# Moving the split operands of every projection to multiples of 128 bytes, and joining the two halves of a row

## The chip, the cores and the metric

The program runs on one core of a Trainium2 chip. That core has five engines that run side by side and meet at semaphores: TensorE (PE, matrix products; its loading of the stationary operand is listed apart as PEld), VectorE (DVE), ScalarE (ACT), GpSimd (POOL) and SyncE (SP), which here only issues DMAs. The metric is the device time of one execution in microseconds; less is better. The kernel before takes 2662.29 us, the median of three runs (2661.83 to 2664.8).

## What is computed

The reference is a two-layer streaming encoder on 256 tokens of width 2048, all in float32. Layer 0 is an RWKV-7 time mixing, layer 1 a chunked band attention on one shared K/V; each is followed by a squared-ReLU MLP, and each sub-layer sits between an RMS norm with a shift and scale made from `c`, and a gate made from `c`.

```
mod = c @ w_ada[layer] + b_ada[layer];  sh1, sc1, gt1, sh2, sc2, gt2 = split(mod, 6)
h = rms_norm(x, g_mix[layer]) * (1 + sc1) + sh1
y = rwkv7_time_mix(h, ...)  if layer == 0  else  chunk_band_attention(h, kp, vp, w_q, w_o, rel_bias)
x = x + gt1 * y
h = rms_norm(x, g_mlp[layer]) * (1 + sc2) + sh2
x = x + gt2 * (square(relu(h @ w_up[layer])) @ w_down[layer])      # 2048 -> 8192 -> 2048
...
return rms_norm(x, g_final)
```

The weights read are 657 MB, and nearly all work is dense products with a 2048-row weight: the time mixing has four (r, k, v, o), the attention four (shared K, shared V, q, o), and each MLP eight times as much as one of these.

## The kernel before

**How a product is made.** Activations lie with the 128 channels of a block on the partitions and the 256 tokens along the row. TensorE reads an operand of the type float32r, which holds a rounded float32; to keep the precision each operand is split into the rounded part H and the rest L, and a product is made as H·aH + H·aL + L·aH. A weight block of 128 by 1024 floats comes by DMA into a tile `raw` (line 372), ScalarE rounds it into `wH` (line 382), and VectorE writes `raw − wH` into `wL` (line 385). The three tiles have 4096 bytes in each partition.

**The split activations** are kept in two kinds of tile. `aHL` (line 421, from `new_hl`) holds all 16 channel blocks (kt = 0 to 15) of one 2048-wide input; the hidden layer of the MLP has one tile `hHL` for each of its blocks (2 by 256 floats, so 2048 bytes). A row of `aHL` is 258 floats (TE = T + 2), because one of its uses, `new_scaled`, puts the shift as two further columns behind the 256 tokens. So in block kt the rounded half begins 2064·kt bytes into the tile, and the low half another 1032 bytes on, 8 bytes behind the end of the rounded half's 256 tokens. `hHL` has no such gap: its low half lies directly behind the rounded one.

**Two ways to multiply.** `proj2` (lines 416 and 417) sends both halves of an activation as one operand of 512 columns past `wH`, and the rounded half again, 256 columns, past `wL`: two multiplications for each kt, called a *pair* here. `proj` (lines 405 to 407) makes three of 256 columns, a *trio*; it is used where one accumulator of 256 columns must do (the time mixing's r and k and the begun part of its output product), and with 258 columns where the shift's column is wanted (the first eight blocks of each MLP and of the shared K). Lines 773 to 775 and 811 to 813 make the same trios for v. Pairs read `aHL` in the MLP's up products, the attention's four products and most of the time mixing's output product, 2816 in all; they read `hHL` in the MLP's down products, 2048 in all. Trios of 256 columns read `aHL` 896 times, those of 258 columns 384 times.

**What sets the order.** Each engine runs its instructions in the order in which the program lists them. The weight DMAs are issued on SP's queue ahead of use into six `raw` buffers; the split weights have three buffers each; the products of a stage follow each other block by block. Between the products VectorE adds up the shift, scale and gate vectors from the tiles `rada` and `raw` (line 458, one 128 by 1024 piece at a time), so in the first MLP and the attention TensorE also does small sums of these (line 480).

**Where tiles lie.** Tiles are placed one behind the other in each partition, in the order in which the pools and tiles are opened, each start rounded up to 32 bytes. The small tile `ct` (the 16 columns of `c`, 64 bytes) is opened near the front, ahead of all large ones except the constants. As the program is placed, the starts are these (bytes, modulo 128):

| tiles | before | after |
|---|---|---|
| `raw`, `wH`, `wL`, `acc`, `rada` (4096 bytes) | 96 | 0 |
| `hHL` (2048 bytes) | 96 | 0 |
| `aHL` (33024 bytes), block kt | 96 + 16·kt, low half 8 more | 0 for both halves; with width 258: 16·kt, low half 8 more |
| tiles of the time mixing's inner work | 32 | 64 |
| `x` and the tiles of the norms outside the time mixing | 96 | 96 |

The stationary operand of kt is 512·(kt mod 8) bytes into its `wH` or `wL` tile, so it has the tile's start modulo 128 too.

Of the kernel before, what the change touches and what calls it, by code (L numbers as in the profile page):

```python
# [12 lines left out]
F32 = mybir.dt.float32  # L13
F32R = mybir.dt.float32r
# [4 lines left out]
P = 128  # L19
D = 2048  # L20
T = 256
KT = D // P
# [7 lines left out]
TE = T + 2  # L30
# [303 lines left out]
class Body:  # L334
# [82 lines left out]
            ins = nc.tensor.matmul(ps[:, 0, :], L[:, i, :], a(kt)[:, 0, :], start=False, stop=(kt == KT - 1))  # L417
        return ins.ins

    def new_hl(self):  # L420
        return self.hp.tile([P, KT, 2, TE], F32R, tag="aHL", bufs=2, name="aHL")


    def ada_src(self, layer, part):
# [131 lines left out]

    def new_scaled(self, sh):
        nc = self.nc
        hl = self.new_hl()
        H, L = hl[:, :, 0, T:TE], hl[:, :, 1, T:TE]  # L560
        s = sh.unsqueeze(2).to_broadcast([P, KT, TE - T])
        nc.scalar.copy(H, s)
        nc.vector.tensor_tensor(out=L, in0=s, in1=H, op=ALU.subtract)
        return hl
# [13 lines left out]
    def run(self):  # L578
        nc, tc, d = self.nc, self.tc, self.d
        ctx = self.ctx  # L580
        gp = self.gp = ctx.enter_context(tc.tile_pool(name="gp", bufs=1))
        self.wp = ctx.enter_context(tc.tile_pool(name="wp", bufs=2))
        nc.scalar.preload_act_table_set("natural_log_exp_and_others")
        self.hp = ctx.enter_context(tc.tile_pool(name="hp", bufs=2))
        self.csts = gp.tile([P, CST.shape[1]], F32, name="csts")
        self.vecs = gp.tile([P, len(VECS), KT], F32, name="vecs")
        self.bada = gp.tile([P, 2 * 96 + 32], F32, name="bada")
        self.ct = gp.tile([P, KT], F32, name="ct")
        nc.scalar.dma_start(out=self.ct, in_=d["c"])
        self.mods = {}  # L590
        for layer in (0, 1, "kv"):
            for part in range(2 if layer == 0 else 0, 2 if layer == "kv" else 6):
                self.mods[(layer, part)] = gp.tile([P, KT], F32, name=f"mod_{layer}_{part}")
        self.mods01 = gp.tile([P, 2, KT], F32, name="mods01")
        for part in range(2):
            self.mods[(0, part)] = self.mods01[:, part, :]
        self.nhalf, self.pool_every = 0, 0
        self.lazy, self.fins, self.ada_pool = False, iter(()), None
        self.ada_done = set()
        self.adas, self.ada_q = self.ada_tiles(), deque()  # L600

        sv, sp = ExitStack(), ExitStack()
        v = self.layer_a(sv, sp)
        with ExitStack() as st:
            self.np = st.enter_context(tc.tile_pool(name="npl", bufs=1, side="right", reuse_waits="tile"))
            xp = st.enter_context(tc.tile_pool(name="xp", bufs=1, side="right", reuse_waits="tile"))
            self.x = xp.tile([P, KT, T], F32, name="x")
            for j in range(KT - 2, KT):
                self.split(self.y_hl, j, v[:, j, :])
            sv.close()  # L610
            self.ada_need((0, 2), (0, 4), (0, 3))
            nxt = self.out_proj(self.pp, "w_o", self.y_hl, (0, 2), "g_mlp0", (0, 4), (0, 3), self.o_ps)
            sp.close()
            with ExitStack() as s2:
                pp = s2.enter_context(tc.tile_pool(name="ps_m0", bufs=2, space=bass.MemoryType.PSUM, reuse_waits="tile"))
                self.psm = lambda: pp.tile([P, 512], F32, tag="m", bufs=2, name="m")
                s2.enter_context(self.ada_room(5))
                nxt = self.mlp(s2, pp, 0, *nxt, "g_kv", ("kv", 1), ("kv", 0))
            with ExitStack() as s2:
                pp = s2.enter_context(tc.tile_pool(name="ps_at", bufs=2, space=bass.MemoryType.PSUM, reuse_waits="tile"))  # L620
                self.psm = lambda: pp.tile([P, 512], F32, tag="m", bufs=1, name="m")
                s2.enter_context(self.ada_room(3))
                o_hl = self.attention(s2, pp, *nxt)
                self.ada_need((1, 2), (1, 4), (1, 3))
                nxt = self.out_proj(pp, "attn_w_o", o_hl, (1, 2), "g_mlp1", (1, 4), (1, 3))
            with ExitStack() as s2:
                pp = s2.enter_context(tc.tile_pool(name="ps_m1", bufs=2, space=bass.MemoryType.PSUM, reuse_waits="tile"))
                self.psm = lambda: pp.tile([P, 512], F32, tag="m", bufs=2, name="m")
                s2.enter_context(self.ada_room(5))
                self.mlp(s2, pp, 1, *nxt)  # L630
                r = self.rstd()
                for lo, hi, eng in ((0, 4, nc.vector), (11, 14, nc.gpsimd), (4, 8, nc.vector), (8, 11, nc.vector),
                                    (14, KT, nc.gpsimd)):
                    x = self.x[:, lo:hi, :]
                    eng.tensor_tensor(out=x, in0=x, in1=r.unsqueeze(1).to_broadcast([P, hi - lo, T]), op=ALU.mult)
                    (nc.sync if eng is nc.vector else nc.scalar).dma_start(out=d["out"][:, lo:hi, :], in_=x)
# [603 lines left out]
```

## Time and profile before

| what | value |
|---|---|
| median of three runs | 2662.29 us (2661.83 to 2664.8) |
| the profiled execution's own time | 2658.25 us |
| its span, first to last instruction | 2656.5 us |
| mean granted TensorE clock | 0.991 |
| TensorE busy | 2577.0 us, 97% |
| VectorE busy | 2094.6 us, 79% |
| ScalarE busy | 1367.6 us, 51% |
| DMA | 663.20 MB, mean 250 GB/s |

The profile comes from one execution, 4 us below the median of the runs. A line of its groups gives the source line, the engine, the operation, the tile written and those read, partitions by elements, the count, the busy time, the mean length of one and the idle time ahead of it with what ended that. Multiplications overlap in the array and their ends are modelled, so the mean lengths of a group (397 ns and 281 ns for the two of a pair) add up to more than the time between one pair and the next; that time is read from the starts in the timeline, or from how many pairs fall into a stretch.

### The profile page before, as it was taken

The numbers are of one execution on the slowest core, as the hardware profiler recorded it, in microseconds if no ns is written. First come the engines' busy times: TensorE is split into PE (matmuls) and PEld (weight loads), VectorE is DVE, ScalarE is ACT, GpSimd is POOL, SyncE is SP. The second block draws the span as 40 slices with busy tenths as digits, with TensorE's granted clock in tenths as the row PEclk, the third lists the DMA queues.
The fourth block names the chain that finished last, engine by engine and source line by source line (L and its number), as shares of the span: only waits on it lengthen the run. The fifth ranks groups of instructions, "written<-read, shape, count | busy, mean of one in ns | idle before, by whom it ended". The sixth has DMA issues, their size and how long they took to land.

```text
span 2656.5 us, 59241 instructions
## 1 busy us (share of the span) xinstructions
PE 2577.0 (97%) x24108; PEld 2253.7 (85%) x24108; DVE 2094.6 (79%) x3054; ACT 1367.6 (51%) x2484; POOL 212.1 (8%) x338
## 2 busy tenths in 40 slices
PE   7999999999999999999999999999999999999997
PEld 4788888888899888888888998877898888888886
DVE  6789878878789888888888898899887556556555
ACT  3346555555456445355365554565564464453554
POOL 1002223223110000000001100000100000000002
PEclk9999999999999999999999999999999999999998
DMA  9876656565768888889998779887766555555553
GB/s 352 311 246 226 203 181 194 184 201 190 248 238 304 328 313 321 328 324 336 325 328 294 238 246 328 316 277 261 264 215 240 188 187 190 190 190 190 185 189 119
DMA packets 207665, 663.20 MB, mean 250 GB/s; under 512 B 21408, under 2 KB 55072, under 8 KB 207392
## 3 DMA queue, kind: packets, MB, share of 16 engines
q1 hardware_dynamic: 205328, 656.89, 71.6%
q8 instruction: 189, 3.10, 0.5%
q10 hardware_dynamic: 2064, 2.53, 0.3%
q14 instruction: 84, 0.69, 0.1%
HBM read 657.23 MB, written 2.10 MB: 248 GB/s over the span
## 4 chain that ended last, share of the span: by engine, by line
PE 81%; DVE 7%; DMA 4%; issue 4%; ACT 2%; POOL 1%; SPq 0%; DVEq 0%; ACTq 0%; POOLq 0%
PE pj L416 42%; PE pj L417 21%; PE pj L405 3%; PE pj L406 3%; PE pj L407 3%; DMA raw<-w_ada 2%; DVE wL L385 2%; DVE acc L458 2%; PE iv L111 1%; PE ms L328 1%; ACT wH L382 1%; DMA raw<-w_o 1%; PE pT L1128 0%; PE o L405 0%; PE m L480 0%
## 5 line engine op out<-in xcount | busy, mean ns | idle before, releaser
L385 DVE TENSOR_TENSOR wL<-raw,wH 128x1024 fp32r<-128x1024 f32 x772 | 942.2, 1222 | 347.0 <-ACT wH L382 340.1
L382 ACT CAST wH<-raw 128x1024 fp32r<-128x1024 f32 x772 | 805.6, 1045 | 761.9 <-PE pj L416 588.9
L416 PE MATMUL pj<-aHL,wH 128*128 128x512 f32 x2816 | 998.1, 397 | 1.4 <-DVE x L953 1.4
L417 PE MATMUL pj<-aHL,wL 128*128 128x256 f32 x2816 | 791.7, 281 | 0.2 <-DVE wL L385 0.2
L416 PE MATMUL pj<-hHL,wH 128*128 128x512 f32 x2048 | 713.8, 395 | 0.0
L416 PEld LDWEIGHTS pj<-aHL,wH 128*128 128x128 f32 x2816 | 532.0, 189 | 129.1 <-issue 8.6
L417 PE MATMUL pj<-hHL,wL 128*128 128x256 f32 x2048 | 568.7, 278 | 0.0
L417 PEld LDWEIGHTS pj<-aHL,wL 128*128 128x128 f32 x2816 | 531.5, 189 | 1.6 <-issue 0.8
L416 PEld LDWEIGHTS pj<-hHL,wH 128*128 128x128 f32 x2048 | 384.1, 188 | 90.1
L417 PEld LDWEIGHTS pj<-hHL,wL 128*128 128x128 f32 x2048 | 384.9, 188 | 0.6 <-DVE wL L385 0.5
L458 DVE SCALAR_TENSOR_TENSOR acc<-rada,ct,acc 128x1024 f32<-128x1024 f32 x256 | 327.9, 1281 | 8.2 <-DMA rada<-w_ada 7.7
L405 PE MATMUL pj<-aHL,wH 128*128 128x256 f32 (+1 forms) x896 | 263.3, 294 | 0.1
L406 PE MATMUL pj<-aHL,wH 128*128 128x256 f32 (+1 forms) x896 | 254.9, 285 | 0.0
L407 PE MATMUL pj<-aHL,wL 128*128 128x256 f32 (+1 forms) x896 | 253.7, 283 | 0.0
L522 POOL TENSOR_TENSOR ss<-ss,sq 128x256 f32<-128x256 f32 x56 | 54.6, 974 | 1579.6 <-ACT sq L521 1579.3
L405 PEld LDWEIGHTS pj<-aHL,wH 128*128 128x128 f32 x896 | 170.7, 190 | 5.0 <-issue 0.5
L407 PEld LDWEIGHTS pj<-aHL,wL 128*128 128x128 f32 x896 | 171.2, 191 | 0.2
L406 PEld LDWEIGHTS pj<-aHL,wH 128*128 128x128 f32 x896 | 170.7, 191 | 0.5
L1024 DVE SCALAR_TENSOR_TENSOR x<-pj,mod,x 128x256 f32<-128x256 f32 x256 | 123.4, 482 | 55.0 <-PE pj L417 51.9
L458 DVE SCALAR_TENSOR_TENSOR acc<-raw,ct,acc 128x1024 f32<-128x1024 f32 x104 | 138.5, 1331 | 19.4 <-DMA raw<-w_ada 19.2
L996 ACT ACTIVATE t<-t 128x256 f32<-128x256 f32 x112 | 46.8, 418 | 124.2 <-DVE t L968 124.2
L998 ACT ACTIVATE t<-t 128x256 f32<-128x256 f32 x128 | 53.4, 417 | 3.4
(252 smaller groups left out, 2818.0 us busy)
## 6 DMA issues: line engine op xcount, KB each, us to landing
raw<-w_up SPq DMA_DIRECT2D x256, 512.0 KB, 4.3
raw<-w_down SPq DMA_DIRECT2D x256, 512.0 KB, 4.3
rada<-w_ada SPq DMA_DIRECT2D x209, 512.0 KB, 5.7
raw<-w_ada SPq DMA_DIRECT2D x111, 512.0 KB, 4.4
rada<-w_ada_kv SPq DMA_DIRECT2D x64, 512.0 KB, 6.6
rawa<-w_ada SPq DMA_DIRECT2D x32, 512.0 KB, 6.8
rawa<-w_ada_t SPq DMA_DIRECT2D x32, 512.0 KB, 7.5
raw<-w_k SPq DMA_DIRECT2D x32, 512.0 KB, 3.8
```

Source lines behind the costliest of these rows:

```text
L382: nc.scalar.copy(Hf, raw)
L385: eng.tensor_tensor(out=Lf, in0=raw, in1=Hf, op=ALU.subtract)
L405: nc.tensor.matmul(ps, H[:, i, :], a(kt)[:, 0, :], start=(first and kt == 0), stop=False)
L406: nc.tensor.matmul(ps, H[:, i, :], a(kt)[:, 1, :], start=False, stop=False)
L407: ins = nc.tensor.matmul(ps, L[:, i, :], a(kt)[:, 0, :], start=False, stop=(last and kt == KT - 1))
L416: nc.tensor.matmul(ps, H[:, i, :], a(kt), start=(kt == 0), stop=False)
L417: ins = nc.tensor.matmul(ps[:, 0, :], L[:, i, :], a(kt)[:, 0, :], start=False, stop=(kt == KT - 1))
L458: nc.vector.scalar_tensor_tensor(out=self.acc, in0=raw, scalar=ck, in1=self.acc, op0=ALU.mult, op1=ALU.add)
L522: (eng or nc.gpsimd).tensor_tensor(out=self.ss, in0=self.ss, in1=sq, op=ALU.add)
L996: nc.scalar.activation(t, t, AF.Relu)
L998: nc.scalar.activation(t, t, AF.Square)
L1024: nc.vector.scalar_tensor_tensor(out=x, in0=ps[:, i, :], scalar=self.mods[(layer, 5)][:, n:n + 1], in1=x, op0=ALU.mult, op1=ALU.add)
```

## The change

`new_hl` takes the width of a row. It is 256 floats unless `new_scaled` asks for 258; the tile has the same size as before (33024 bytes), with the rows of 256 packed into its front. So the low half lies directly behind the rounded half, and the two halves of a block are one run of 2048 bytes. `ct` becomes 24 floats wide (96 bytes), of which the first 16 are used, so every tile that is opened after it moves up by 32 bytes, and the large ones start at the multiples of 128 that the table shows. Nothing else changes: on each engine the same instructions stand in the same order with the same waits, and every operand has the same number of elements; what differs is where the operands lie.

```diff
-    def new_hl(self):
-        return self.hp.tile([P, KT, 2, TE], F32R, tag="aHL", bufs=2, name="aHL")
+    def new_hl(self, width=T):
+        t = self.hp.tile([P, KT * 2 * TE], F32R, tag="aHL", bufs=2, name="aHL")
+        return t[:, :KT * 2 * width].rearrange("p (k i t) -> p k i t", i=2, t=width)
...
     def new_scaled(self, sh):
         nc = self.nc
-        hl = self.new_hl()
+        hl = self.new_hl(TE)
...
-        self.ct = gp.tile([P, KT], F32, name="ct")
+        self.ct = gp.tile([P, KT + 8], F32, name="ct")[:, :KT]
```

## The prediction

> **What bounds the kernel now.** I read the page first: the busy times, the slices and the costliest groups, then the stretches of single stages, then the timeline of TensorE inside one of them.
>
> ```profile
> span 2656.5 us, 59241 instructions
> PE 2577.0 (97%) x24108; PEld 2253.7 (85%) x24108; DVE 2094.6 (79%) x3054; ACT 1367.6 (51%) x2484; POOL 212.1 (8%) x338
> PE   7999999999999999999999999999999999999997
> PEclk9999999999999999999999999999999999999998
> ```
>
> TensorE is busy in nine tenths or more of every slice but the first and the last, at nearly its full clock. What stands in front of a multiplication is in the groups:
>
> ```profile
> L416 PE MATMUL pj<-aHL,wH 128*128 128x512 f32 x2816 | 998.1, 397 | 1.4 <-DVE x L953 1.4
> L417 PE MATMUL pj<-aHL,wL 128*128 128x256 f32 x2816 | 791.7, 281 | 0.2 <-DVE wL L385 0.2
> L416 PE MATMUL pj<-hHL,wH 128*128 128x512 f32 x2048 | 713.8, 395 | 0.0
> L417 PE MATMUL pj<-hHL,wL 128*128 128x256 f32 x2048 | 568.7, 278 | 0.0
> ```
>
> These are the 4864 pairs, and in total 1.6 us of waiting stands ahead of them. So for most of the span only one thing counts: how far apart the multiplications start. No instruction is added, removed or moved by this change; if the time moves, it is because an operand at another address is read or written at another speed. The trace of before holds two natural experiments on that, since the rows of `aHL` start at sixteen different places and those of `hHL` at one.
>
> The first is the second MLP, whose stages do nothing but pairs. The rows give the stretch, its length and the busy time and count of each engine. Up, down, up and down follow each other:
>
> ```profile
> core 0: us, PE busy (x) PEld busy (x) DVE busy (x) ACT busy (x) POOL busy (x), PEclk, DMA share, GB/s
> 2103.50:2193.20 89.70, 89.70 (x514) 78.38 (x513) 50.07 (x64) 53.27 (x92) 0.00 (x0) 1.00 0.56 188
> 2193.20:2282.05 88.85, 88.85 (x514) 77.62 (x513) 53.99 (x65) 34.88 (x36) 0.00 (x0) 1.00 0.57 190
> 2282.05:2371.78 89.73, 89.73 (x514) 78.43 (x513) 50.08 (x64) 53.28 (x92) 0.00 (x0) 1.00 0.56 188
> 2371.78:2460.63 88.85, 88.85 (x514) 77.63 (x513) 53.98 (x65) 34.87 (x36) 0.00 (x0) 1.00 0.56 190
> ```
>
> Each stage is 256 pairs (512 multiplications and one or two at the cut) with TensorE busy throughout. An up stage, which reads `aHL`, takes 89.73 us, or 350.5 ns a pair; a down stage, which reads `hHL`, takes 88.85 us, or 347.1 ns. Same weights' tiles, same number of columns, 3.4 ns apart.
>
> The second is inside an up stage. This is the timeline of TensorE over one weight block of 16 kt; the first row is kt 0, and the others shown are, in order, kt 2, 3, 4 (both of its multiplications), 5, 6, 7, 10, 11, 14, 15 (both), and kt 0 of the next block:
>
> ```profile
> 2304.51 0.39 PE L416 MATMUL pj<-aHL,wH 128*128 128x512 f32 x1
> ...
> 2305.20 0.39 PE L416 MATMUL pj<-aHL,wH 128*128 128x512 f32 x1
> ...
> 2305.55 0.39 PE L416 MATMUL pj<-aHL,wH 128*128 128x512 f32 x1
> ...
> 2305.90 0.39 PE L416 MATMUL pj<-aHL,wH 128*128 128x512 f32 x1
> 2306.12 0.28 PE L417 MATMUL pj<-aHL,wL 128*128 128x256 f32 x1
> 2306.24 0.40 PE L416 MATMUL pj<-aHL,wH 128*128 128x512 f32 x1
> ...
> 2306.60 0.40 PE L416 MATMUL pj<-aHL,wH 128*128 128x512 f32 x1
> ...
> 2306.95 0.40 PE L416 MATMUL pj<-aHL,wH 128*128 128x512 f32 x1
> ...
> 2308.01 0.40 PE L416 MATMUL pj<-aHL,wH 128*128 128x512 f32 x1
> ...
> 2308.37 0.40 PE L416 MATMUL pj<-aHL,wH 128*128 128x512 f32 x1
> ...
> 2309.42 0.40 PE L416 MATMUL pj<-aHL,wH 128*128 128x512 f32 x1
> ...
> 2309.78 0.39 PE L416 MATMUL pj<-aHL,wH 128*128 128x512 f32 x1
> 2310.01 0.28 PE L417 MATMUL pj<-aHL,wL 128*128 128x256 f32 x1
> 2310.12 0.39 PE L416 MATMUL pj<-aHL,wH 128*128 128x512 f32 x1
> ```
>
> The block takes 5.61 us, 350.6 ns a pair, but not evenly: kt 0 to 4 take 2306.24 − 2304.51 = 1.73 us, 346 ns each; kt 5 to 10 take 2308.37 − 2306.24 = 2.13 us, 355 ns each; kt 11 to 15 take 1.75 us, 350 ns each. The engines beside TensorE do not know of kt, so where a row starts matters by some ten nanoseconds a pair, in no order that I can read off as a plain rule of multiples.
>
> **The change, part by part.**
>
> *Rows of `aHL` become runs of 2048 bytes at one alignment.* This is what `hHL` is already: both halves joined, every row at the same place against the stationary operand of its kt. Before, an `aHL` row starts 16 bytes further along against its weights with each kt; after, the distance is the same for all, and it is the one that `hHL` has before and after. So I take the down stage's 347.1 ns for the pairs that read `aHL`: 2816 × 3.44 ns = 9.7 us. It lies on the path in full, since TensorE has no cover there: it is the bound, and nothing else waits to take its place (VectorE is busy 50 of 90 us in these stages; where it is busiest its row is below).
>
> *Trios of 256 columns*, 896 of them, get the same joined rows. The timeline has three such starts in a quiet moment of the time mixing:
>
> ```profile
> 515.57 0.28 PE L405 MATMUL pj<-aHL,wH 128*128 128x256 f32 x1
> 515.69 0.28 PE L406 MATMUL pj<-aHL,wH 128*128 128x256 f32 x1
> 515.81 0.28 PE L407 MATMUL pj<-aHL,wL 128*128 128x256 f32 x1
> 515.93 0.28 PE L405 MATMUL pj<-aHL,wH 128*128 128x256 f32 x1
> ```
>
> That is 360 ns a trio. The trace has no trio on joined rows. The nearest row is the pair's, 1% (3.44 of 350.5); so 3.5 ns × 896 = 3.1 us, with ends of 3.1 us worse (the low half's own multiplication may as well lose) and 6.2 us better (it may gain twice, being the one whose start moves most).
>
> *The 384 trios of 258 columns* keep rows of 258, which move against their weights as before: nothing, ± 1% of 384 × 0.36 us, so ± 1.4 us.
>
> *All large tiles move by 32 bytes.* This shifts moving and stationary operands together. No pair in the trace has weights at another start, so the price is unknown, and bounded from both sides by the slow and fast places of the `aHL` rows (rivals, below). I take nothing: kt 2 and 10 have the rounded half of `aHL` at a multiple of 128 already, and their starts lie 0.35 and 0.36 us ahead of the next, no better than the block's mean.
>
> *Writes of the split activations, the weights' splitting, DMA.* The rows of ScalarE and VectorE that write a joined row and a gapped one:
>
> ```profile
> L999 DVE TENSOR_TENSOR hHL<-t,hHL 128x256 fp32r<-128x256 f32 x128 | 53.9, 421 | 1.0 <-ACT t L998 0.8
> L576 DVE TENSOR_TENSOR aHL<-mix,aHL 128x256 fp32r<-128x256 f32 x32 | 13.4, 421 | 0.0
> 868.50:958.30 89.80, 89.80 (x631) 78.46 (x621) 81.26 (x93) 34.97 (x36) 0.00 (x0) 1.00 0.89 321
> 0.00:200.00 200.00, 168.27 (x1459) 134.02 (x1460) 150.05 (x289) 76.08 (x126) 14.81 (x22) 0.97 0.88 303
> ```
>
> 421 ns both: nothing. VectorE's other work changes its addresses by 32 bytes alike; TensorE covers it, with 8.5 us to spare in the busiest stage, a down stage of the first MLP (third row). DMA is nearest to a bound in the first 200 us, at 0.88 of its engines (last row), where its tiles go from 32 to 64 modulo 128: nothing, ± 1%, so ± 2 us.
>
> Sum: 9.7 + 3.1 = 12.8 us. The profiled execution of 2658.25 us would come to 2645.5, and the median of the runs, which stands 4.0 us above it, 2662.3 − 12.8 = **2649.5 us**, faster by 0.48%. Differences within 0.2% (5.3 us) are what a measurement here can't tell from no change.
>
> **The rivals.**
>
> *B, nothing moves.* The 3.4 ns between up and down could belong to the stage and not to the address: ScalarE is busy 53.3 us in an up stage and 34.9 in a down stage. Then the time stays at 2662. Against it stands the unevenness by kt. The Trainium skill (SBUF — State Buffer, Specifications) says that SBUF has lines of 16 bytes and that two hits in a line suffice for the full rate. By that rule no start here costs anything, since even a low half 8 bytes into a line takes two floats from it, and B would hold; the kt's of 346 and 355 ns do not agree with it as the whole story.
>
> *C, the 32 bytes help as well.* Multiplications then also save a part of their reading because rows and weights begin on a boundary. What speaks for it: between the fastest starts in the rows above, 0.22 us (kt 4, 2305.90 to 2306.12) for 512 columns and 0.11 us (kt 15, 2310.01 to 2310.12) for 256, a pair would take 330 ns, 17 ns under the down stage. Over all 4864 pairs that is 83 us beyond A, 2566 us; TensorE would still be the bound, as 256 × 0.33 = 84 us is above VectorE's 81.3. Against it: rows that begin on multiples of 128 show no gain now. I take half of the price, since no row is nearer to either end: 2608 us. The Trainium skill (TensorE: Matmul & The Clock Gate, Back-to-back issue gap) gives 2.5 ns over the columns' time at 2.4 GHz, 216 ns for 512 columns and 109 for 256; by it a pair would take 325 ns and C's full price be 107 us, an estimate from that page, which no pair in this trace reaches.
>
> *D, slower: boundaries are the bad places.* The rows of `aHL` whose rounded half begins on a multiple of 64 are kt 2, 6, 10 and 14; their pairs take 0.35, 0.35, 0.36 and 0.36 us, 355 ns in the mean, and the other twelve (5.61 − 1.42) / 12 = 349 ns. If it is the absolute start that counts, and not that against the weights, the change puts every row there: 2816 × 4.5 ns = 12.7 us, and for the down products 2048 × 7.9 ns = 16.2 us, together 28.9 us, 2691 us. It decides against the change as soon as a pair at the new start takes more than the present mean of both kinds, 349.1 ns, and shows beyond the 0.2% from 350.2 ns. Against it: kt 5, 8 and 9 lie in the slow stretch too and are no such multiples.
>
> **How the numbers follow.** A, the forecast, 0.42: two stages that differ in little but the rows speak for it, and its price is read, not guessed. C 0.24, B 0.13, D 0.21. All of A and C is faster by over 0.2%: 0.66; same 0.13; slower 0.21. A alone spans 2643 (9.7 us, the trios' better end of 6.2 and the 3.4 us of the ± terms) to 2657, above which the gain would not show. The range has to reach into C and D: at 2590 some 0.08 of C's upper price is left out below, at 2690 some 0.10 of D above.
>
> **What the profile after would show.** Right: the four stretches above become alike, near 88.85 us each; in an up stage the starts of one block's pairs are even, 0.35 us at every kt; the group L416 on `aHL` falls from 397 to 395 ns and L417 from 281 to 278; counts, waits and the lengths on VectorE and ScalarE stay. C: the down stages shorten too. D: they lengthen, to 91 us. B: 89.7 and 88.85 stay, with even starts. The prediction is wrong above all if the down stages move at all, for I priced the shift of 32 bytes at nothing.

## The result, and the profile after

The changed kernel takes 2665.77 us in the median of 22 runs (2656.06 to 2674.16), the kernel before on the same chips 2662.44 us (22 runs, 2655.56 to 2667.42). The ratio is 1.0012, with a 95% interval of 1.0003 to 1.0021: no change, by the 0.2% that a measurement here can tell, and if anything a little slower. The forecast of 2649.5 us did not come.

The page of the kernel after, with its groups of pairs (line 416 makes the 512 columns, line 417 the 256):

```profile
span 2657.1 us, 59241 instructions
PE 2576.0 (97%) x24108; PEld 2255.4 (85%) x24108; DVE 2096.7 (79%) x3054; ACT 1369.0 (52%) x2484; POOL 215.7 (8%) x338
L416 PE MATMUL pj<-aHL,wH 128*128 128x512 f32 x2816 | 998.2, 398 | 1.4 <-DVE x L954 1.4
L417 PE MATMUL pj<-aHL,wL 128*128 128x256 f32 x2816 | 791.4, 281 | 0.0
L416 PE MATMUL pj<-hHL,wH 128*128 128x512 f32 x2048 | 715.3, 394 | 0.0
L417 PE MATMUL pj<-hHL,wL 128*128 128x256 f32 x2048 | 573.7, 280 | 0.1
```

Counts and waits are as before, and so is the sum. But the stages do not look like it. The second MLP, down, up and down (a stage is 256 pairs; one more multiplication is caught at each cut):

```profile
2197.91:2286.75 88.84, 88.84 (x514) 78.23 (x513) 54.04 (x65) 35.06 (x36) 0.00 (x0) 1.00 0.57 190
2286.75:2375.50 88.75, 88.75 (x514) 78.25 (x513) 50.02 (x64) 53.28 (x92) 0.00 (x0) 1.00 0.57 190
2375.50:2464.34 88.84, 88.84 (x514) 78.23 (x513) 54.02 (x65) 35.05 (x36) 0.00 (x0) 1.00 0.57 190
```

The up stage fell from 89.73 to 88.75 us, as forecast. In the first MLP, though, the same pairs run at two speeds. Both rows are 128 pairs (eight weight blocks), the first from the end of a down stage into an up stage, the second from the same up stage, with one round of small sums between them:

```profile
937.09:981.46 44.37, 44.37 (x258) 39.12 (x257) 40.70 (x46) 20.89 (x28) 0.00 (x0) 1.00 0.97 360
999.05:1044.27 45.22, 45.22 (x258) 39.24 (x257) 40.81 (x47) 27.85 (x48) 0.00 (x0) 1.00 0.96 359
```

The first stretch takes 346.7 ns a pair, the second 353.3. The pace did not change where the down stage ended; it changed at the sums. VectorE and DMA are busy alike in both, and the granted clock is 1.00 in both. The timeline of TensorE shows what the difference is, first in the fast stretch, then in the slow one:

```profile
942.30 0.39 PE L416 MATMUL pj<-hHL,wH 128*128 128x512 f32 x1
942.53 0.28 PE L417 MATMUL pj<-hHL,wL 128*128 128x256 f32 x1
942.64 0.39 PE L416 MATMUL pj<-hHL,wH 128*128 128x512 f32 x1
942.87 0.28 PE L417 MATMUL pj<-hHL,wL 128*128 128x256 f32 x1
942.99 0.39 PE L416 MATMUL pj<-hHL,wH 128*128 128x512 f32 x1
...
943.34 0.39 PE L416 MATMUL pj<-hHL,wH 128*128 128x512 f32 x1
```

```profile
1004.36 0.40 PE L416 MATMUL pj<-aHL,wH 128*128 128x512 f32 x1
1004.59 0.28 PE L417 MATMUL pj<-aHL,wL 128*128 128x256 f32 x1
1004.71 0.40 PE L416 MATMUL pj<-aHL,wH 128*128 128x512 f32 x1
1004.94 0.28 PE L417 MATMUL pj<-aHL,wL 128*128 128x256 f32 x1
1005.05 0.40 PE L416 MATMUL pj<-aHL,wH 128*128 128x512 f32 x1
1005.30 0.28 PE L417 MATMUL pj<-aHL,wL 128*128 128x256 f32 x1
1005.42 0.40 PE L416 MATMUL pj<-aHL,wH 128*128 128x512 f32 x1
```

Three pairs take 943.34 − 942.30 = 1.04 us in the one and 1005.42 − 1004.36 = 1.06 us in the other, again and again until something interrupts: two **rhythms**. In the fast one the starts of all pairs are alike (in whole nanoseconds 230 from the 512 columns to the 256, and 116 or 117 on to the next pair). In the slow one they repeat every three pairs, 233, 241 and 236 ns after the 512 columns. Between two interruptions every stretch of joined rows in this trace keeps one of the two from end to end. The output products, most of the attention and part of the first MLP are slow here, the second MLP is all fast; together the pairs that read `aHL` come to 350.7 ns in the mean of their starts, against 350.6 before. So what the even rows gained in one stage they lost in others.

The slow rhythm is no product of the change. It stands in the trace of before too, where `hHL` already had joined rows; 64 pairs each, in the fourth down stage of the first MLP:

```profile
1428.63:1450.82 22.19, 22.19 (x130) 19.39 (x129) 22.19 (x26) 10.96 (x16) 3.81 (x4) 1.00 0.85 285
1473.50:1496.11 22.61, 22.61 (x130) 19.60 (x129) 17.94 (x21) 11.70 (x16) 3.23 (x4) 1.00 0.72 242
```

That is 346.7 and 353.3 ns again, and the last down stage of all was slow as well. (The fast one is not quite the same here: the pairs of the first row are 350 and 343 ns apart in turn. A stretch is called fast or slow below by its mean.) The rows of `aHL` before the change, whose places move by 16 bytes with each kt, never held either: 350.5 ns by the mean of every long stretch.

### The profile page after: what moved, and what is told of

The parts are those of the page before. It is cut to its first block, busy times and chain, and to the rows that moved or that the text cites. A ratio compares the mean times of both kernels' runs of the same rounds, so it can differ in the third digit from the quotient of the medians.

```text
span 2657.1 us, 59241 instructions
## 1 busy us (share of the span) xinstructions
PE 2576.0 (97%) x24108; PEld 2255.4 (85%) x24108; DVE 2096.7 (79%) x3054; ACT 1369.0 (52%) x2484; POOL 215.7 (8%) x338
## 3 DMA queue, kind: packets, MB, share of 16 engines
q10 hardware_dynamic: 2064, 2.53, 0.3%
## 4 chain that ended last, share of the span: by engine, by line
PE 80%; DVE 8%; issue 4%; DMA 4%; ACT 2%; POOL 1%; DVEq 0%; ACTq 0%; SPq 0%; POOLq 0%
PE pj L416 41%; PE pj L417 21%; PE pj L405 3%; PE pj L406 3%; PE pj L407 3%; DMA raw<-w_ada 2%; DVE wL L385 2%; DVE acc L459 2%; PE iv L111 1%; ACT wH L382 1%; PE o L405 1%; PE ms L328 1%; DMA rada<-w_ada 0%; PE m L481 0%; PE pT L1129 0%
## 5 line engine op out<-in xcount | busy, mean ns | idle before, releaser
L997 ACT ACTIVATE t<-t 128x256 f32<-128x256 f32 x112 | 46.9, 418 | 122.8 <-DVE t L969 122.8
L1000 DVE TENSOR_TENSOR hHL<-t,hHL 128x256 fp32r<-128x256 f32 x128 | 53.7, 420 | 1.7 <-ACT t L999 0.9
```

Source lines behind the costliest of these rows:

```text
L997: nc.scalar.activation(t, t, AF.Relu)
L1000: nc.vector.tensor_tensor(out=h[:, 1, :], in0=t, in1=h[:, 0, :], op=ALU.subtract)
```

## The experiments

In the expectations, theory 1 was that joined rows are read in one of two lasting rhythms that an interruption sets anew, wherever the tiles begin; theory 2 that it is the shift by 32 bytes which brings the slow one.

**Each part alone, and the change once more.** Rows joined, tiles where they were:

```diff
     def new_hl(self, width=T):
...
-        self.ct = gp.tile([P, KT + 8], F32, name="ct")[:, :KT]
+        self.ct = gp.tile([P, KT], F32, name="ct")
```

> Rows joined, but the tiles where they were before (96 modulo 128). Theory 1 (joined rows are read in one of two lasting rhythms, 346.7 or 353.3 ns a pair, taken anew after each interruption, whatever the alignment): stretches of aHL pairs show both rhythms, as in the changed kernel, and the ratio to the kernel before is 0.998 to 1.003. Theory 2 (the shift by 32 bytes brings the slow rhythm, joined rows alone do not): every aHL stretch at 346.7 ns, hHL as before, 10 to 12 us faster, ratio 0.995 to 0.996.

The ratio was 1.0003 (0.9986 to 1.0021; 12 runs, 2653.62 to 2675.57). Its second MLP, down, up and down:

```profile
2196.56:2285.40 88.84, 88.84 (x514) 78.23 (x513) 54.02 (x65) 35.06 (x36) 0.00 (x0) 1.00 0.55 190
2285.40:2374.15 88.75, 88.75 (x514) 78.25 (x513) 50.02 (x64) 53.23 (x92) 0.00 (x0) 1.00 0.54 190
2374.15:2464.57 90.42, 90.42 (x514) 78.46 (x513) 53.96 (x65) 34.92 (x36) 0.00 (x0) 1.00 0.53 186
```

One kernel, one execution, two down stages: 88.84 and 90.42 us for the same 256 pairs. Rows of `aHL` were slow too, though no tile had been shifted; here are 128 pairs of the time mixing's output product, at 353.3 ns:

```profile
821.72:866.94 45.22, 45.22 (x258) 39.08 (x256) 40.77 (x47) 27.19 (x46) 0.00 (x0) 1.00 0.93 351
```

So theory 2 falls. The shift alone (the kernel before with the small tile of 24 floats):

> Tiles at 0 modulo 128, rows of aHL with the gap of 8 bytes as before. Theory 1: aHL pairs at 350.5 ns in the mean with their unevenness by kt, hHL stretches nearly all at 346.7 as before, ratio 0.999 to 1.001. Theory 2: several hHL stretches at 353.3 ns, 5 to 13 us slower, ratio 1.002 to 1.005.

Ratio 0.9998 (0.9987 to 1.0008), the same time as before, and `aHL` at 89.72 us a stage as before; but in this execution nearly all stretches of `hHL` were slow, where theory 1 expected them fast; down and up:

```profile
2196.48:2286.90 90.42, 90.42 (x514) 78.34 (x513) 53.90 (x65) 34.91 (x36) 0.00 (x0) 1.00 0.54 186
2286.90:2376.62 89.72, 89.72 (x514) 78.41 (x513) 50.07 (x64) 53.27 (x92) 0.00 (x0) 1.00 0.54 188
```

That is what theory 2 expected of the trace, but not its time, and the version with joined rows alone has slow stretches without the shift. One trace of each cannot tell a rhythm that comes with the tiles' places from one that differs between executions; the changed kernel, run again, can:

> The changed kernel, a second profiled execution. If a stretch's rhythm is fixed by the program, the same stretches run at 353.3 ns as in the first (the output products, both halves of the attention, three of the first MLP's seven that are longest). If it is drawn in each execution, another set, with 0 to 100% of the pairs in the slow rhythm: all 4864 slow would be 32 us above all fast.

The median was 2669.72 us, the ratio 1.0021 (1.0010 to 1.0031). This time every stretch was slow but eight of the attention's short ones (16 pairs each), the second MLP too, and the span was 2672.1 us against 2657.1 in the first trace of the same kernel; down and up:

```profile
2204.77:2295.22 90.45, 90.45 (x514) 78.43 (x513) 53.85 (x65) 34.91 (x36) 0.00 (x0) 1.00 0.53 186
2295.22:2385.68 90.46, 90.46 (x514) 78.40 (x513) 50.13 (x64) 53.24 (x92) 0.00 (x0) 1.00 0.53 186
```

The rhythm differs between executions, so a single profile says nothing of which one a kernel will have. The granted clock does not explain the spread of the runs: of the 22 runs of the change that stand above, the eight with a clock of 0.993 took between 2656.06 and 2671.78 us.

**What makes a rhythm last.** Rows joined, but each 2064 bytes behind the last:

```diff
-        return t[:, :KT * 2 * width].rearrange("p (k i t) -> p k i t", i=2, t=width)
+        t = t.rearrange("p (k w) -> p k w", k=KT)[:, :, :2 * width]
+        return t.rearrange("p k (i t) -> p k i t", i=2)
```

> The change, with the two halves of a row joined but each row 2064 bytes behind the last, so that rows again start 16 bytes further along for each kt. If it is the even place of the rows that lets a rhythm last: aHL pairs at one mean near 350.5 ns in every stretch, uneven by kt as before the change, never 346.7 or 353.3. If it is the joining: stretches at 346.7 and 353.3 as in the changed kernel.

All stretches of `aHL` ran at 352.1 ns, uneven by kt from 345 to 360 ns, and none at 346.7 or 353.3, while `hHL` in the same trace had both (one run, 2663.65 us). An up stage:

```profile
2286.87:2377.02 90.15, 90.15 (x514) 78.54 (x513) 50.09 (x64) 53.30 (x92) 0.00 (x0) 1.00 0.53 187
```

So it is the even place of the rows against the weights that lets a rhythm last; joining the halves alone does not, and gave 352.1 ns where rows with the gap have 350.5. A second test interrupts the pairs where nothing did:

```diff
+        def kick(n):
+            if layer and n % 4 == 0:
+                nc.tensor.matmul(self.psm()[:, :1], self.cst("ident"), self.col(C_ONE), start=True, stop=True)
...
+            if q:
+                kick(f)
...
+                kick(n)
```

> The change, with one small product of one column (its output is not used) ahead of every fourth block in the second MLP from its first down products on, so every 64 pairs, where nothing interrupted the pairs before. If a rhythm is taken at an interruption and kept to the next: the second MLP falls into stretches of 64 pairs, each all at 346.7 or all at 353.3 ns, with both kinds among them. If something else sets it (an execution as a whole, the load on the other engines): all stretches of the second MLP alike.

The one run took 2677.18 us. Of the 28 stretches that begin behind such a product, 27 began slow. A short wait early in each of the four down stages changed the rhythm as well, once to the slow one and three times to the fast one, which then lasted to the next small product. The rows are 31 pairs ahead of one small product and 47 behind it:

```profile
2215.65:2226.39 10.74, 10.74 (x64) 9.39 (x63) 6.76 (x8) 4.20 (x4) 0.00 (x0) 1.00 0.58 202
2232.61:2249.22 16.61, 16.61 (x96) 14.40 (x95) 10.13 (x12) 6.29 (x6) 0.00 (x0) 1.00 0.55 189
```

That is 346 and 353 ns: an interruption can change the rhythm, and stretches beside each other differ, so it does not belong to an execution as a whole. But it is no even draw either. What decides at the interruption was not found.

**The distance between moving and stationary operand.** The unevenness by kt suggests that this distance matters. Rows and weights lie tens of kilobytes apart; what is called their distance here is the difference of their starts modulo 256 bytes, which is the same for all even rows and all weights. A small tile ahead of `aHL` moves both kinds of activations on (and the tiles behind them) and leaves the weights (8, 16, 24, 32 or 40 floats for 32 to 160 bytes):

```diff
         self.hp = ctx.enter_context(tc.tile_pool(name="hp", bufs=2))
+        self.nc.vector.memset(self.hp.tile([P, 8], F32, tag="gap", bufs=1, name="gap"), 0.0)
```

> The change, and the split activations 64 bytes further than the weights (64 modulo 128 against 0; one small memset more). Theory 1 with rhythms set by TensorE alone: both 346.7 and 353.3 ns again, ratio 0.998 to 1.003. If the distance between moving and stationary operand sets the rhythm (as the unevenness by kt suggests): other lengths than these two, one for all stretches, between 343 and 357 ns, so between 18 us faster and 32 us slower.

> The change, and the split activations 32 bytes further than the weights. If the distance sets the lengths of the rhythms: a pair of lengths other than 346.7 and 353.3, as 64 bytes gave 348.9 and 353.3. If not: these two again.

> The change, and the split activations 128 bytes further than the weights. As for 32 bytes; where the lengths come back to 346.7 and 353.3, the distance counts modulo 128 only.

> The change with a distance of 96 bytes. If the distance counts modulo 64: one rhythm of 346.7 ns as with 32. If not: one of its own, between 343 and 357 ns as 0, 64 and 128 bytes gave.

> The change with a distance of 160 bytes. If the distance counts modulo 128: one rhythm of 346.7 ns as with 32. 128 bytes gave 351.1 where 0 gave 346.7 and 353.3, so I expect a length of its own.

| distance, bytes | ns a pair, by stretch | time, us |
|---|---|---|
| 0 (the change) | 346.7 and 353.3 | 2665.77, ratio 1.0012 |
| 32 | 346.7 in all | one run 2646.34; timed below |
| 64 | 348.9 and 353.3 | 2664.38, ratio 0.9995 (0.9982 to 1.0009) |
| 96 | 350.1 in all | one run 2659.66 |
| 128 | 351.1 in all | one run 2662.80 |
| 160 | 346.7 in all | one run 2641.96 |

So the distance sets which rhythms there are. 64 bytes has two and not the one length that was expected, 32 bytes one and not a new pair, and 160 bytes no length of its own; neither 64 nor 128 bytes is a period (0 and 64 differ, 0 and 128 differ). For 96, 128 and 160 bytes there is one trace each, so a second rhythm that this execution did not take is not ruled out. At 32 and at 160 bytes only the fast one was seen. The first was timed, once as it is and once with the small tile as before the change, so that weights begin at 96 modulo 128:

> The same kernel as the one with 32 bytes of distance, timed. If the one rhythm of 346.7 ns that all its stretches showed belongs to the distance: it is there in this execution too, ratio 0.993 to 0.996, and the runs spread less than those of the changed kernel (18 us). If that execution was a lucky draw: stretches at 353.3 ns again, ratio 0.997 to 1.003.

> Joined rows, 32 bytes further than the weights, but with the small tile as before the change, so that weights stay at 96 and the rows come to 0 modulo 128. If only the distance counts: all stretches at 346.7 ns, ratio 0.993 to 0.996, as with the weights at 0. If multiples of 128 for the weights count: stretches at 353.3 ns or another length, ratio from 0.997.

The ratios were 0.9928 (0.9912 to 0.9945; 6 runs, 2636.10 to 2646.65) and 0.9924 (0.9909 to 0.9939; 6 runs, 2635.01 to 2645.28): faster than the kernel before by 0.7%, with runs 10 to 11 us apart at most instead of 18, and the same with the weights at 0 and at 96. Weights at 0 and at 96 have now both been run at both distances: at 0 bytes each shows the two rhythms, at 32 bytes each shows the fast one alone. Multiples of 128 bytes are worth nothing here. The page of the first, and its second MLP:

```profile
span 2641.6 us, 59242 instructions
L416 PE MATMUL pj<-aHL,wH 128*128 128x512 f32 x2816 | 987.7, 393 | 1.3 <-DVE x L955 1.3
L416 PE MATMUL pj<-hHL,wH 128*128 128x512 f32 x2048 | 711.6, 391 | 0.0
2182.40:2271.23 88.83, 88.83 (x514) 78.67 (x513) 53.98 (x65) 34.94 (x36) 0.00 (x0) 1.00 0.54 190
2271.23:2359.98 88.75, 88.75 (x514) 78.68 (x513) 50.00 (x64) 53.23 (x92) 0.00 (x0) 1.00 0.54 190
```

Every stretch of the three traces at 32 bytes, in the first MLP as in the second, lies at 346.7 ns. Last, the distance without the joining (the kernel before with the small tile ahead of `aHL`):

> The kernel before (rows of 2064 bytes, small tile as it was) with the split activations 32 bytes further than the weights, so that only the distance is changed. If the joined rows carry part of the gain of the version with both: aHL pairs stay near 350.5 ns and uneven by kt, hHL pairs are all at 346.7, and the ratio lies between 0.995 and 0.999. If the distance alone does it: aHL pairs at 346.7 too, ratio near 0.993.

Ratio 0.9980 (0.9968 to 0.9992). Down and up in its second MLP:

```profile
2193.89:2282.73 88.84, 88.84 (x514) 78.66 (x513) 53.92 (x65) 34.92 (x36) 0.00 (x0) 1.00 0.54 190
2282.73:2372.44 89.71, 89.71 (x514) 78.42 (x513) 50.09 (x64) 53.27 (x92) 0.00 (x0) 1.00 0.53 188
```

All `hHL` stretches are fast and `aHL` stays at 350.4 ns. So the distance is worth 0.2%, and the packing of the rows (halves joined, all at one place), once the rhythm is sure, over 0.5% more. The kernel that differs from this one in the packing alone is the one with the weights at 96: 0.9980 − 0.9924 = 0.0056, or 15 us.

## Why the prediction was wrong

**What bounds the kernel**: right. In all traces TensorE is busy for 97% of the span, the pairs wait for a few microseconds in all, and the differences between kernels lie in the distance between starts.

**Joined rows run at the down stage's pace**: the step that failed. Its words were "So I take the down stage's 347.1 ns for the pairs that read `aHL`". The second MLP's down stages were read as what even rows cost; they were one of two rhythms, and the other, 353.3 ns, stood in the same trace in the first MLP's fourth down stage and in the last one of all, which the prediction did not use. Two alike down stages close to each other were one case seen twice. In its place the runs showed 346.7 or 353.3 ns by stretch: the first trace after had 350.7 ns for `aHL` in the mean and the second 353.0, against 350.6 before.

**The price of joining**: right in size where the rhythm is fast, 12.8 us forecast and 15 us between the kernel with the distance alone and that with both. What the forecast missed is that at the distance of the change the fast rhythm is not sure. The part on the 256-column trios was 3.1 us; by the starts on line 405's trios that nothing interrupts, they went from 356.6 to 358.5 ns in the trace after, a loss of 1.7 us for 896 of them (within the end of 3.1 us), and to 352.2 ns at a distance of 32 bytes, a gain of 3.9 us.

**The shift of 32 bytes at nothing**: right (the shift alone at 0.9998, and the last version at 0.9924 without it and 0.9928 with it). The sentence that the prediction would be wrong above all if the down stages moved held in its letter, as they did move in the first MLP, but not for the reason given.

**The trios of 258 columns, writes and DMA at nothing**: right; the trios stay at 360.0 ns in both traces, and the groups of VectorE and ScalarE are as before.

**The rivals.** B came out in the time, but not by its reason: 53 against 35 us of ScalarE made no difference, for up and down stages take the same where both are fast. C and D both took the absolute start for the cause. Rows on a multiple of 128 ran in both rhythms at a distance of 0 and in the fast one alone at 32, and the two versions at 32 bytes, one with the rows at 0 and one with the rows at 32 modulo 128, took the same time; so neither holds. C's 330 ns was also too low a reading: in whole nanoseconds its two starts lie 227 and 114 ns apart, 341 ns together, which would have made its full price some 30 us and not 83. D's figure of 355 ns lay near the slow rhythm, by chance as far as the runs show. The rule of the Trainium skill on lines of 16 bytes (SBUF — State Buffer, Specifications), by which, as the prediction read it, no start here costs anything, does not account for these runs: 32 bytes of distance between two operands, both on multiples of 32, change a pair from 353.3 to 346.7 ns. The prediction's estimate of 325 ns for a pair, worked out from the Trainium skill (TensorE: Matmul & The Clock Gate, Back-to-back issue gap), was reached in no run; the fastest lasting pair was 346.7 ns.

## What to carry to other kernels

Where one engine runs back to back, read its pace from the starts and over all stages before taking one stage's pace as a price, and look for stretches of equal work at two speeds. A gain that rests on a rhythm has to be tried in several executions; here a spread of 18 us among the runs of the change told more than its median. Try a few distances between the moving and the stationary operand: 32 bytes were worth more than the whole change, and made it pay.

## What the runs showed of the hardware that was not expected

With equal distance of all rows from their weights, back-to-back float32r multiplications settled into a rhythm that lasted for up to hundreds of pairs, to the next interruption. There were two rhythms at a distance of 0 bytes (346.7 and 353.3 ns a pair of 512 and 256 columns) and at 64 (348.9 and 353.3), and one at 32 (346.7, three traces), 96 (350.1), 128 (351.1) and 160 (346.7; one trace each). Every pair slow against every pair fast would be 4864 × 6.6 ns = 32 us; the spans of the second trace of the change and of the timed version with 32 bytes are 2672.1 − 2641.6 = 30.5 us apart. The tiles `raw` moved together with the weights in every run, so that it is the distance to the weights that counts, and not to `raw`, is argued and not shown. Why the distance matters, and why 32 and 160 bytes have one rhythm alone, is open.
